# A Conformer convolution inside a decoder trunk: first weights split ahead and kept in DRAM, tap matrices from the host, fewer TensorE taps

## The chip, the cores and the metric

The kernel runs on one core of one Trainium2 chip. The time is device microseconds of one execution; a kernel's time is the median of several executions. Five engines run beside each other: TensorE (PE, with its weight loads shown as PEld), VectorE (DVE), ScalarE (ACT), GpSimd (POOL) and SyncE (SP), which here only issues DMAs. ACT and POOL issue DMAs too.

## The reference, cut to what matters

Two layers over 512 tokens of width 1024: a Mamba-2 mixer (SSD), then a Conformer convolution module, each followed by a gated MLP with a causal convolution of width 3. The Conformer module is what the change is about:

```python
def conformer_conv(x, pw1_w, pw1_b, dw_w, dw_b, ln_g, ln_b, pw2_w, pw2_b):
    h = jax.nn.glu(x @ pw1_w + pw1_b, axis=-1)      # 1024 -> 2 x 1024
    h = causal_dwconv(h, dw_w, dw_b)                # 31 taps per channel
    h = jax.nn.silu(layer_norm(h, ln_g, ln_b))
    return h @ pw2_w + pw2_b                        # 1024 -> 1024
```

## The kernel before, in words

Activations lie channels by tokens: eight tiles of 128 channels x 512 tokens. Every product is made of three fp32r matmuls: weights and activations are split into a high part (rounded to fp32r) and a low part (the rest), and high x high, low x high and high x low are added up in PSUM (lines 275 to 277, in `mm_unit`).

Weights come as a stream of 440 units (`weight_units`), each two 128-row blocks of 256 columns. `Weights._make` (line 101) loads raw fp32 by a DMA on SP (line 110, 512 KB for two units), rounds the high part on POOL (line 115) and subtracts it on DVE for the low part (line 116). There are three raw buffers and five pairs of high and low tiles; `get` makes four units ahead of the one in use. One unit is twelve matmuls.

The order of the work: SSD, first conv FFN (`ffn(0)`: 22 up-projections of four units, in three parts, with the down-projections of each part behind it), Conformer, second FFN. The program is written in that order, and a scheduler at build time, which simulates a timeline, settles the order of instructions in each engine's queue and puts in the waits. On the chip each queue is then worked off in that order.

The Conformer (line 660 on) goes over eight channel tiles p:

- `taps(p)` (line 673) builds on DVE the small diagonal matrices with which TensorE makes taps 1 to 4J of the causal convolution, J = `PE_J[p]` (4, 4, 5, 5, 5, 5, 5, 6). They lie in half of a buffer (`ab`) of the SSD.
- `mm_pair("pw1", p, ...)` makes both halves of the GLU: 48 matmuls.
- `glu(p)` (line 685) evacuates them (`scaled`, line 304, two DVE operations), makes the sigmoid on ACT and the product `ta` on DVE (line 688). For TensorE's taps it needs four copies of `ta` that are shifted by 0 to 3 tokens: for p below 7 `ta` goes to DRAM and comes back in four DMAs from POOL's queue (lines 691 and 693); for p = 7 sixteen copies on ACT and DVE make it (lines 699 to 705). Taps 0 and above 4J are made on ACT (lines 709, 710) and DVE (line 713, one operation a tap), and added (line 716).
- `dwconv(p)` (line 719) runs TensorE's taps: for each j four matmuls of 128 x 32 in fp32, each two records in the trace (line 723). Then DVE adds them (line 728), subtracts the mean of tile 0 (line 735), and adds the tile to the sums `s1` (line 741) and of squares (line 258). It is called three tiles late, behind the last unit of pw1 of tile p + 3; the last four, tiles 4 to 7, lie behind the last pw1 matmuls.

Then three idle matmuls (line 757) keep TensorE busy, sixteen records of one-column matmuls turn the two sums (line 762), the statistics are spread over the partitions (`across`, line 767), and the second pointwise product (pw2) begins.

Of the kernel before, what the change touches and what calls it, by code (L numbers as in the profile page):

```python
# [10 lines left out]
F32 = mybir.dt.float32  # L11
F32R = mybir.dt.float32r
AF = mybir.ActivationFunctionType
ALU = mybir.AluOpType
# [3 lines left out]
P = 128  # L18
T = 512
# [7 lines left out]
CK = 31  # L27
NCH = 4
RMS_EPS = 1e-6
LN_EPS = 1e-5  # L30
PE_J = (4, 4, 5, 5, 5, 5, 5, 6)
MAX_J = 7
FPARTS = ((0, 8), (8, 16), (16, 22))

_COLS = {}
# [1 line left out]
for _name, _w in (  # L37
# [3 lines left out]
    ("fb1", 44), ("wt", 8 * MAX_J * 4),  # L41
):
    _COLS[_name] = _n
    _n += _w
# [47 lines left out]
class Weights:  # L92
    def __init__(self, nc, src, raw, split, look):
        self.nc, self.src, self.raw, self.split, self.look = nc, src, raw, split, look
        self.seq = weight_units()
        self.made = 0
        self.used = 0
        self.ready = deque()
        self.cur = None

    def _make(self):
        nc = self.nc
        kind, p, k = self.seq[self.made]
        if self.cur is None or self.cur[0] != (kind, p) or not self.cur[1] <= k < self.cur[2]:
            n = 1
            while n < (2 if self.made > 1 else 1) and self.made + n < len(self.seq) and self.seq[self.made + n] == (kind, p, k + 2 * n):
                n += 1
            t = self.raw.tile([P, 4, 256], F32, name="wraw", tag="wraw")
            s = self.src[kind][p]
            nc.sync.dma_start(t[:, 0 : 2 * n, :], s[:, k : k + 2 * n, :])  # L110
            self.cur = ((kind, p), k, k + 2 * n, t)
        t = self.cur[3][:, k - self.cur[1] : k - self.cur[1] + 2, :]
        hi = self.split.tile([P, 2, 256], F32R, name="whi", tag="whi")
        lo = self.split.tile([P, 2, 256], F32R, name="wlo", tag="wlo")
        nc.gpsimd.tensor_scalar(hi, t, 1.0, 1.0, op0=ALU.mult, op1=ALU.mult)  # L115
        nc.vector.tensor_tensor(lo, t, hi, op=ALU.subtract)  # L116
        self.ready.append((hi, lo))
        self.made += 1
# [13 lines left out]
def trunk(ctx, tc, a, out):  # L132
    nc = tc.nc
    pe, act, dve, pool = nc.tensor, nc.scalar, nc.vector, nc.gpsimd
# [8 lines left out]
    dr = ctx.enter_context(tc.tile_pool(name="dr", bufs=1, space=DRAM))  # L143
# [59 lines left out]
    def col(name, i, n=1):  # L203
        c = _COLS[name] + i
        return par[:, c : c + n]
# [99 lines left out]
            us.append(u)  # L305
        return us

    # ---------------------------------------------------------------- SSD
    sq = SqSum()
    xs = []  # L310
    dps = c_tile()
# [303 lines left out]
        ps = mm_pair("out", p, ysplit, 8, 16)  # L615
        out_evac(p, ps)

    # ---------------------------------------------------------------- conv FFN
    def ffn(i, finish, last=None):
        fx, fsq = hs["xs"], hs["sq"]  # L620
        box = {}

        def get_r():
            box["r"] = fsq.rstd(D)

        for pi, (pa, pb) in enumerate(FPARTS):
            acts = Acts()
            for p in range(pa, pb):
                ps = mm_pair(f"up{i}", p, fx, hooks={3: get_r} if p == 0 else None)
                us = scaled(ps, box["r"])  # L630
                os_ = []
                for u, j in zip(us, (p, NF + p)):
                    o = cv_tile()
                    act.activation(o, u, AF.Identity, scale=col(f"fw{i}", 3 * j + 2), bias=col(f"fb{i}", j))  # L634
                    os_.append(o)
                for d in (1, 2):
                    for u, o, j in zip(us, os_, (p, NF + p)):
                        dve.scalar_tensor_tensor(  # L638
                            o[:, d:], in0=u[:, : T - d], scalar=col(f"fw{i}", 3 * j + 2 - d), in1=o[:, d:],
                            op0=ALU.mult, op1=ALU.add,  # L640
                        )
                act.activation(os_[0], os_[0], AF.Silu)  # L642
                dve.tensor_tensor(os_[0], os_[0], os_[1], op=ALU.mult)  # L643
                acts.add(os_[0])
            for p in range(4):
                if last and pb == NF and p == 3:
                    last(acts, pa, pb)
                    break
                ps = mm_pair(f"dn{i}", p, acts, pa, pb)
                for m in range(2):  # L650
                    dve.tensor_tensor(h[2 * p + m], h[2 * p + m], ps[m], op=ALU.add)  # L651
                if pi == len(FPARTS) - 1:
                    if p == 0:
                        hs["sq"], hs["xs"] = SqSum(), []
                    for m in range(2):
                        finish(2 * p + m)

    ffn(0, lambda m: h_done(m, lambda i: col("nm1", i)))

    # ---------------------------------------------------------------- Conformer  # L660
    cx, csq = hs["xs"], hs["sq"]
    gd = [dr.tile([P, 4 + T], F32, name=f"gd{i}") for i in range(3)]
    for t in gd:
# [6 lines left out]
    ys = []  # L670
    m0s1 = wt("xdt", (P, NCH, 256), bufs=1).rearrange("p c e -> p (c e)")

    def taps(p):
        n = 4 * PE_J[p]
        if p % 3 == 0:
            box["wd"] = ab_tile().rearrange("p h t -> p (h t)")
        c = (p % 3) * 2 * T
        wd = box["wd"][:, c : c + 32 * n].rearrange("p (n e) -> p n e", e=32)
        dve.tensor_tensor(
            wd, mask32.unsqueeze(1).broadcast_to([P, n, 32]),  # L680
            col("wt", 4 * MAX_J * p, n).unsqueeze(2).broadcast_to([P, n, 32]), op=ALU.mult,
        )
        return wd

    def glu(p, ps, wd):
        ta, tb = scaled(ps, box["r"])
        act.activation(tb, tb, AF.Sigmoid, bias=col("p1b", 8 + p))
        dve.scalar_tensor_tensor(ta, in0=ta, scalar=col("p1b", p), in1=tb, op0=ALU.add, op1=ALU.mult)
        t = ap_.tile([P, 4, T], F32, name="as", tag="as")
        if p < 7:  # L690
            nc.gpsimd.dma_start(gd[p % 3][:, 4:], ta)
            for s in range(4):
                nc.gpsimd.dma_start(
                    t[32 * s : 32 * s + 32], gd[p % 3][:, s : s + T].rearrange("(b c) t -> c b t", b=4)
                )
        else:
            for s in range(4):
                dve.memset(t[32 * s : 32 * s + 32, :, 0 : 4 - s], 0.0)
            for b in range(4):
                for s in range(4):  # L700
                    o, i = t[32 * s : 32 * s + 32, b, 4 - s :], ta[32 * b : 32 * b + 32, : T - 4 + s]
                    if s % 2:
                        act.activation(o, i, AF.Copy)
                    else:
                        dve.tensor_copy(o, i)
        acc = [cv_tile(), u_tile()]
        dw = lambda d: col("dw", CK * p + CK - 1 - d)
        d2 = 4 * PE_J[p] + 1
        act.activation(acc[0], ta, AF.Identity, scale=dw(0), bias=col("dwb", p))
        act.activation(acc[1][:, d2:], ta[:, : T - d2], AF.Copy, scale=dw(d2))  # L710
        for i, d in enumerate(range(d2 + 1, CK)):
            o = acc[i % 2]
            dve.scalar_tensor_tensor(  # L713
                o[:, d:], in0=ta[:, : T - d], scalar=dw(d), in1=o[:, d:], op0=ALU.mult, op1=ALU.add
            )
        dve.tensor_tensor(acc[0][:, d2:], acc[0][:, d2:], acc[1][:, d2:], op=ALU.add)
        return p, t, wd, acc[0]

    def dwconv(p, t, wd, acc):
# [9 lines left out]
        if p == 0:  # L729
# [2 lines left out]
            m0 = m0s1[:, 0:T]  # L732
            act.activation(m0, mp, AF.Copy, scale=1.0 / P)
            box["m0"] = m0
        dve.tensor_tensor(y, y, box["m0"], op=ALU.subtract)
        if p == 0:
            box["s1"] = m0s1[:, T : 2 * T]
            act.activation(box["s1"], y, AF.Copy)
            box["sq"] = SqSum()
        else:  # L740
            dve.tensor_tensor(box["s1"], box["s1"], y, op=ALU.add)
        box["sq"].add(y)
        ys.append(y)

    pend = deque()
    for p in range(8):
# [10 lines left out]
    idle(3)  # L757

    stp = c_tile()
    for i, t in enumerate((box["s1"], box["sq"].t)):  # L760
        for c in range(NCH):
            pe.matmul(
                stp[:, 4 * i + c : 4 * i + c + 1], lhsT=t[:, c * P : (c + 1) * P], rhs=ones[:, 0:1],
                start=True, stop=True,
            )

    def across(v):
# [150 lines left out]
def _layout(i):  # L918
# [15 lines left out]
    for l in range(2):  # L934
# [2 lines left out]
    o["pw1"] = _pairs(f["b_pw1_w"][0], [(P * p, D + P * p) for p in range(8)])  # L937
    o["pw2"] = _pairs(f["b_pw2_w"][0], seq4)
    dww = f["b_dw_w"][0]
    taps = dww[CK - 1 - np.arange(1, 4 * MAX_J + 1)].reshape(MAX_J, 4, 8, 4, 32)[:, ::-1]  # L940
    parts = {
        "nm0": _chan(f["norm_mix"][0]), "nm1": _chan(f["norm_mix"][1]),
        "nf0": _chan(f["norm_ffn"][0]), "nf1": _chan(f["norm_ffn"][1]),
# [4 lines left out]
        "lng": _chan(f["b_ln_g"][0]), "lnb": _chan(f["b_ln_b"][0]), "p2b": _chan(f["b_pw2_b"][0]),  # L948
        "fw0": _taps(f["f_conv_w"][0]), "fb0": _chan(f["f_conv_b"][0]),
        "fw1": _taps(f["f_conv_w"][1]), "fb1": _chan(f["f_conv_b"][1]),  # L950
        "wt": taps.transpose(1, 4, 2, 0, 3).reshape(P, -1),
    }
    o["par"] = np.ascontiguousarray(np.concatenate([parts[k] for k in _COLS], axis=1))
    o["g0"] = np.ascontiguousarray(parts["nm0"])
# [22 lines left out]
```

## Time and profile before

| what | us |
|---|---|
| median of three runs (1345.31 to 1346.75) | 1346.13 |
| span of the profiled execution, first to last instruction | 1344.2 |
| the difference, taken as what lies around the span | 1.9 |
| TensorE busy in that span | 1325.3 (99%) |
| VectorE busy | 1006.6 (75%) |
| ScalarE busy | 407.7 (30%) |
| GpSimd busy | 360.8 (27%) |

The profile is of one execution. Busy time of TensorE is taken from matmuls whose ends are modelled, so its 99% does not say that each stretch is bounded by it; where in the span something else sets the pace is read from the timelines of a stretch. DVE operations overlap by a little: from start to start of two that follow each other is less than the duration of one.

### The profile page before, as it was taken

To read this page: it belongs to the slowest core of one execution; us is meant where nothing else is said; L and a number is where in the kernel's file an instruction comes from. 1 tells how busy PE (TensorE), PEld (TensorE's weight loads), DVE (VectorE), ACT (ScalarE), POOL (GpSimd) and SP (SyncE) were. 2 spreads that over 40 slices of the span, in tenths; PEclk is the share of its full clock that TensorE was granted. 3 is DMA by queue.
4 is the path that set the end of the run, shared out by engine and by line. 5 is a ranking of instruction groups with operands and counts; after the bars stand their busy time and mean duration, and the time that the engine had idled before them with its cause. 6 is when DMAs were issued, how large, how long until landed. Compare 5 with 4: busy or idle time off the path is not lost.

```text
span 1344.2 us, 17019 instructions
## 1 busy us (share of the span) xinstructions
PE 1325.3 (99%) x6312; PEld 1069.5 (80%) x6312; DVE 1006.6 (75%) x1505; ACT 407.7 (30%) x653; POOL 360.8 (27%) x479
## 2 busy tenths in 40 slices
PE   8999999999999999999999999998999999999998
PEld 5778888888888888888888887645888888888887
DVE  7879987388989975477457779998787637763774
ACT  4575644055312321022002331225232202210224
POOL 3213222222223222222222225430222222222220
PEclk9999999999999999999999999998999999999999
DMA  6334432243233333223322336540323322232232
GB/s 215 115 125 157 157 125 94 79 138 114 95 111 108 110 95 94 94 97 100 101 95 86 100 104 188 152 131 17 110 91 98 94 95 94 96 108 94 94 87 71
DMA packets 43795, 145.55 MB, mean 108 GB/s; under 512 B 5953, under 2 KB 6337, under 8 KB 42689
## 3 DMA queue, kind: packets, MB, share of 16 engines
q1 hardware_dynamic: 40336, 135.28, 31.4%
q0 software_dynamic: 2800, 9.18, 2.7%
q8 instruction: 50, 0.82, 0.3%
q14 instruction: 33, 0.26, 0.1%
q10 hardware_dynamic: 576, 0.01, 0.0%
HBM read 140.37 MB, written 4.07 MB: 107 GB/s over the span
## 4 chain that ended last, share of the span: by engine, by line
PE 81%; DVE 12%; DMA 2%; issue 2%; ACT 2%; SPq 0%; POOL 0%; DVEq 0%; ACTq 0%; POOLq 0%
PE mm L277 26%; PE mm L275 26%; PE mm L276 25%; DVE cv L713 2%; DVE u L713 2%; DVE wlo L116 2%; DVE cv L401 1%; DMA wraw<-in_dram 1%; DMA ab<-acs_d 1%; PE pc L477 1%; DVE u L304 1%; ACT ab L444 1%; PE pc L500 1%; PE pc L473 1%; DVE sqs L258 0%
## 5 line engine op out<-in xcount | busy, mean ns | idle before, releaser
L115 POOL TENSOR_SCALAR whi<-wraw 128x512 fp32r<-128x512 f32 x440 | 340.7, 775 | 929.0 <-PE mm L277 623.9
L116 DVE TENSOR_TENSOR wlo<-wraw,whi 128x512 fp32r<-128x512 f32 x440 | 308.9, 705 | 238.6 <-POOL whi L115 237.8
L275 PE MATMUL mm<-xs,whi 128*128 128x512 f32 x1216 | 476.3, 393 | 1.1 <-POOL whi L115 0.6
L276 PE MATMUL mm<-xs,wlo 128*128 128x512 f32 x1216 | 474.4, 391 | 0.2 <-DVE wlo L116 0.2
L277 PE MATMUL mm<-xs,whi 128*128 128x512 f32 x1216 | 473.3, 391 | 0.5 <-DVE xs L222 0.5
L275 PEld LDWEIGHTS mm<-xs,whi 128*128 128x128 f32 x1216 | 228.2, 188 | 54.7 <-POOL whi L115 4.6
L276 PEld LDWEIGHTS mm<-xs,wlo 128*128 128x128 f32 x1216 | 228.2, 188 | 50.0 <-issue 1.8
L277 PEld LDWEIGHTS mm<-xs,whi 128*128 128x128 f32 x1216 | 228.0, 188 | 50.1 <-DVE xs L222 1.6
L275 PE MATMUL mm<-as,whi 128*128 128x512 f32 x532 | 207.0, 390 | 0.7 <-ACT as L242 0.7
L276 PE MATMUL mm<-as,wlo 128*128 128x512 f32 x532 | 206.8, 389 | 0.0
L277 PE MATMUL mm<-as,whi 128*128 128x512 f32 x532 | 203.8, 390 | 0.6 <-DVE as L244 0.6
L634 ACT ACTIVATE cv<-u,par 128x512 f32<-128x512 f32 x88 | 67.1, 809 | 360.9 <-DVE u L304 360.9
L638 DVE SCALAR_TENSOR_TENSOR cv<-u,par,cv 128x511 f32<-128x511 f32 (+1 forms) x176 | 136.4, 835 | 0.0
L304 DVE TENSOR_TENSOR u<-mm,rstd 128x512 f32<-128x512 f32 x152 | 102.1, 686 | 29.3 <-PE mm L277 29.3
L275 PEld LDWEIGHTS mm<-as,whi 128*128 128x128 f32 x532 | 99.9, 188 | 22.0 <-issue 1.2
L277 PEld LDWEIGHTS mm<-as,whi 128*128 128x128 f32 x532 | 99.8, 188 | 21.9 <-DVE as L244 1.0
L276 PEld LDWEIGHTS mm<-as,wlo 128*128 128x128 f32 x532 | 99.9, 188 | 20.5
L401 DVE SCALAR_TENSOR_TENSOR cv<-u,par,cv 128x511 f32<-128x511 f32 (+2 forms) x96 | 76.3, 820 | 3.1 <-ACT cv L397 2.8
L642 ACT ACTIVATE cv<-cv 128x512 f32<-128x512 f32 x44 | 27.8, 633 | 81.3 <-DVE cv L638 81.3
L651 DVE TENSOR_TENSOR h<-h,mm 128x512 f32<-128x512 f32 x46 | 30.8, 686 | 24.6 <-PE mm L277 24.6
L218 ACT ACTIVATE as<-cv 128x512 fp32r<-128x512 f32 x44 | 27.9, 634 | 67.7 <-DVE cv L643 67.7
L444 ACT ACTIVATE ab<-ab,acT 128x128 f32<-128x128 f32 x128 | 38.9, 389 | 15.5 <-DMA ab<-acs_d 15.5
(181 smaller groups left out, 943.4 us busy)
## 6 DMA issues: line engine op xcount, KB each, us to landing
wraw<-up_dram SPq DMA_DIRECT2D x88, 512.0 KB, 3.6
wraw<-in_dram SPq DMA_DIRECT2D x47, 512.0 KB, 3.7
wraw<-dn_dram SPq DMA_DIRECT2D x40, 512.0 KB, 3.6
wraw<-pw_dram SPq DMA_DIRECT2D x24, 512.0 KB, 3.7
ab<-acs_d SPq DMA_DIRECT2D x8, 1024.0 KB, 4.9
wraw<-out_dram SPq DMA_DIRECT2D x16, 512.0 KB, 3.9
as<-gd POOLq DMA_DIRECT2D x28, 256.0 KB, 5.5
ab<-nac_d SPq DMA_DIRECT2D x32, 128.0 KB, 5.9
```

What stands on the lines that cost most here:

```text
L115: nc.gpsimd.tensor_scalar(hi, t, 1.0, 1.0, op0=ALU.mult, op1=ALU.mult)
L116: nc.vector.tensor_tensor(lo, t, hi, op=ALU.subtract)
L275: pe.matmul(ps[m], lhsT=whi[:, kk, c], rhs=xhi, start=(k + kk == k0), stop=False)
L276: pe.matmul(ps[m], lhsT=wlo[:, kk, c], rhs=xhi, start=False, stop=False)
L277: pe.matmul(ps[m], lhsT=whi[:, kk, c], rhs=xlo, start=False, stop=(k + kk == k1 - 1))
L304: dve.tensor_tensor(u, q, r, op=ALU.mult)
L401: dve.scalar_tensor_tensor(o[:, d:], in0=u[:, : T - d], scalar=col("cw", 4 * i + 3 - d), in1=o[:, d:], op0=ALU.mult, op1=ALU.add,)
L444: act.activation(e, e, AF.Relu, bias=acT[:, c, 4 * g + j : 4 * g + j + 1], scale=-1.0)
L634: act.activation(o, u, AF.Identity, scale=col(f"fw{i}", 3 * j + 2), bias=col(f"fb{i}", j))
L638: dve.scalar_tensor_tensor(o[:, d:], in0=u[:, : T - d], scalar=col(f"fw{i}", 3 * j + 2 - d), in1=o[:, d:], op0=ALU.mult, op1=ALU.add,)
L651: dve.tensor_tensor(h[2 * p + m], h[2 * p + m], ps[m], op=ALU.add)
L713: dve.scalar_tensor_tensor(o[:, d:], in0=ta[:, : T - d], scalar=dw(d), in1=o[:, d:], op0=ALU.mult, op1=ALU.add)
```

## The change

- `PE_J` becomes (4, 4, 4, 4, 4, 4, 4, 5): 33 instead of 39 steps of four tap matmuls on TensorE; the other taps go to DVE (line 713).
- `presplit`: during the first FFN, behind its tiles 5 to 21, sixteen parts of pw1's weights (512 KB each) are loaded into the SSD's `ab` buffers, split on ACT (high) and DVE (low), and written to DRAM from POOL's queue, 1 MB a part. In the Conformer, `_make` then loads high and low directly, two DMAs of 256 KB a unit on SP, with no work on POOL and DVE.
- `taps(p)` loads the diagonal matrices, made on the host, by a DMA from POOL's queue instead of building them on DVE.
- The shifted copies of tile 7 are sixteen DMAs on SP from SBUF to SBUF.
- The mean of tile 0 is subtracted before TensorE's taps are added for p above 2 (line 735's operation moves into `glu`), and tile 7 is left out of the two sums: four more matmuls each on the tile and on its square take their place.

```diff
-PE_J = (4, 4, 5, 5, 5, 5, 5, 6)
+PE_J = (4, 4, 4, 4, 4, 4, 4, 5)
...
+        if kind in self.split_src:
+            pair = []
+            for q, name in enumerate(("whi", "wlo")):
+                t = self.split.tile([P, 2, 256], F32R, name=name, tag=name)
+                nc.sync.dma_start(t.rearrange("p k c -> p (k c)").bitcast(F32), self.split_src[kind][p][:, k // 2, q, :])
+                pair.append(t)
+            self.ready.append(tuple(pair))
+            self.made += 1
+            return
...
+    def presplit(kind, n):
+        W.split_src[kind] = [dr.tile([P, 4, 2, T], F32, name=f"{kind}s{p}", tag=f"{kind}s{p}") for p in range(n)]
+        parts = [(p, k) for p in range(n) for k in (0, 4)]
+        b = None
+        for i in range(len(parts) + 1):
+            prev = b
+            if i < len(parts):
+                p, k = parts[i]
+                b = ab_tile()
+                nc.sync.dma_start(b[:, 0:2, :].rearrange("p u (k c) -> p (u k) c", k=2), a[kind][p][:, k : k + 4, :])
+            if prev is not None:
+                p, k = parts[i - 1]
+                o = prev[:, 2:6, :].rearrange("p (u q) t -> p u q t", q=2)
+                r = o.bitcast(F32R)
+                for u in range(2):
+                    act.activation(r[:, u, 0, :], prev[:, u, :], AF.Copy)
+                    dve.tensor_tensor(r[:, u, 1, :], prev[:, u, :], r[:, u, 0, :], op=ALU.subtract)
+                nc.gpsimd.dma_start(W.split_src[kind][p][:, k // 2 : k // 2 + 2], o)
+            yield
...
+        ahead = presplit("pw1", 8) if i == 0 else iter(())
...
+                if p > 4:
+                    next(ahead, None)
...
-        dve.tensor_tensor(
-            wd, mask32.unsqueeze(1).broadcast_to([P, n, 32]),
-            col("wt", 4 * MAX_J * p, n).unsqueeze(2).broadcast_to([P, n, 32]), op=ALU.mult,
-        )
+        nc.gpsimd.dma_start(wd, a["wd"][:, 128 * sum(PE_J[:p]) : 128 * sum(PE_J[: p + 1])])
...
-                dve.memset(t[32 * s : 32 * s + 32, :, 0 : 4 - s], 0.0)
-            for b in range(4):
-                for s in range(4):
-                    o, i = t[32 * s : 32 * s + 32, b, 4 - s :], ta[32 * b : 32 * b + 32, : T - 4 + s]
-                    if s % 2:
-                        act.activation(o, i, AF.Copy)
-                    else:
-                        dve.tensor_copy(o, i)
+                pool.memset(t[32 * s : 32 * s + 32, :, 0 : 4 - s], 0.0)
+            for s in range(4):
+                for b in range(4):
+                    nc.sync.dma_start(t[32 * s : 32 * s + 32, b, 4 - s :], ta[32 * b : 32 * b + 32, : T - 4 + s])
...
+        if p > 2:
+            dve.tensor_tensor(acc[0], acc[0], box["m0"], op=ALU.subtract)
...
-        dve.tensor_tensor(y, y, box["m0"], op=ALU.subtract)
+        if p < 3:
+            dve.tensor_tensor(y, y, box["m0"], op=ALU.subtract)
...
-        else:
+        elif p < 7:
             dve.tensor_tensor(box["s1"], box["s1"], y, op=ALU.add)
-        box["sq"].add(y)
+        if p < 7:
+            box["sq"].add(y)
...
-    for i, t in enumerate((box["s1"], box["sq"].t)):
+    sq7 = wt("sq", bufs=2)
+    act.activation(sq7, ys[7], AF.Square)
+    for j, t in enumerate((box["s1"], box["sq"].t, ys[7], sq7)):
```

## Rows read from the trace of the kernel before

**Rows 1.** The page's head: span and number of instructions.
```profile
span 1344.2 us, 17019 instructions
```
**Rows 2.** Busy time by stretch: PE, PEld, DVE, ACT, POOL, clock, DMA share, GB/s.
```profile
405.00:783.00 378.00, 378.00 (x1668) 312.62 (x1667) 266.50 (x383) 80.15 (x118) 102.15 (x139) 1.00 0.31 98
783.00:890.00 107.00, 107.00 (x534) 76.79 (x532) 100.21 (x141) 23.92 (x34) 46.48 (x62) 1.00 0.55 151
```
**Rows 3.** Timeline of PE: start, us, line, operation, tiles, shape, count.
```profile
889.73 0.39 PE L277 MATMUL mm<-xs,whi 128*128 128x512 f32 x1
890.04 8.66 PE L723 MATMUL pc<-as,ab 128*32 128x512 f32 x80
...
912.54 2.84 PE L175 MATMUL mm<-con,ones 128*128 128x512 f32 x6
919.35 1.36 PE L762 MATMUL pc<-ones,xdt 128*128 128x1 f32 x8 [3.97 <-DVE xdt L741]
920.57 1.84 PE L762 MATMUL pc<-ones,sqs 128*128 128x1 f32 x8
```
**Rows 4.** Timeline of DVE in the Conformer.
```profile
799.68 1.27 DVE L304 TENSOR_TENSOR u<-mm,rstd 128x512 f32<-128x512 f32 x2
801.94 0.75 DVE L688 SCALAR_TENSOR_TENSOR u<-u,par 128x512 f32<-128x512 f32 x1
803.57 1.36 DVE L713 SCALAR_TENSOR_TENSOR cv<-u,par,cv 128x494 f32<-128x494 f32 x1 [0.89 <-ACT cv L709]
804.86 0.72 DVE L713 SCALAR_TENSOR_TENSOR u<-u,par 128x493 f32<-128x493 f32 x1
805.50 0.72 DVE L713 SCALAR_TENSOR_TENSOR cv<-u,par,cv 128x492 f32<-128x492 f32 x1
...
896.43 0.68 DVE L304 TENSOR_TENSOR u<-mm,rstd 128x512 f32<-128x512 f32 x1
...
901.37 0.74 DVE L688 SCALAR_TENSOR_TENSOR u<-u,par 128x512 f32<-128x512 f32 x1
...
919.23 0.69 DVE L258 TENSOR_TENSOR sqs<-sqs,sq 128x512 f32<-128x512 f32 x1
```
**Rows 5.** Groups of DVE instructions from 783 to 922 us.
```profile
L713 DVE SCALAR_TENSOR_TENSOR cv<-u,par,cv 128x486 f32<-128x486 f32 (+6 forms) x42 | 34.2, 823 | 0.9 <-ACT cv L709 0.9
L116 DVE TENSOR_TENSOR wlo<-wraw,whi 128x512 fp32r<-128x512 f32 x33 | 23.6, 719 | 5.7 <-POOL whi L115 5.7
L705 DVE COPY as<-u 32x508 f32<-32x508 f32 (+1 forms) x8 | 3.3, 415 | 0.1
L679 DVE TENSOR_TENSOR ab<-con,par 128x640 f32<-128x640 f32 (+1 forms) x2 | 2.0, 1022 | 0.0
```
**Rows 6.** Timeline of POOL: a rounding beside the long DVE operation of rows 4.
```profile
803.77 0.63 POOL L115 TENSOR_SCALAR whi<-wraw 128x512 fp32r<-128x512 f32 x1
```
**Rows 7.** Groups of instructions of the whole span.
```profile
L219 DVE TENSOR_TENSOR as<-cv,as 128x512 fp32r<-128x512 f32 x44 | 30.4, 691 | 0.8 <-ACT as L218 0.7
L218 ACT ACTIVATE as<-cv 128x512 fp32r<-128x512 f32 x44 | 27.9, 634 | 67.7 <-DVE cv L643 67.7
L437 PEld LDWEIGHTS pc<-con,cv 128*128 128x128 f32 x64 | 7.4, 141 | 0.3
```
**Rows 8.** Timeline of SP: four loads issued one behind the other.
```profile
5.60 2.08 SPq L190 DMA_DIRECT2D cv<-x_dram  x4
```
**Rows 9.** DMA issues: KB each, median us to landing (820 to 880 us; whole span).
```profile
as<-gd POOLq DMA_DIRECT2D x16, 256.0 KB, 5.3
...
y_dram<-u SPq DMA_DIRECT2D x8, 256.0 KB, 2.3
```
**Rows 10.** DMA queues from 820 to 880 us: packets, MB, share of 16 engines.
```profile
q0 software_dynamic: 1810, 5.91, 39.3%
q1 hardware_dynamic: 1150, 4.19, 24.8%
```
**Rows 11.** Busy time by stretch, columns as in rows 2: the clock around the statistics.
```profile
920.00:922.00 2.00, 2.00 (x11) 2.00 (x11) 0.00 (x0) 0.50 (x1) 0.00 (x0) 0.50 0.00 0
```

More of the change, by code (lines that the diff above doesn't have):

```diff
@@ L30 @@
 LN_EPS = 1e-5
-PE_J = (4, 4, 5, 5, 5, 5, 5, 6)
-MAX_J = 7
+PE_J = (4, 4, 4, 4, 4, 4, 4, 5)
 FPARTS = ((0, 8), (8, 16), (16, 22))
@@ L40 @@
     ("lng", 8), ("lnb", 8), ("p2b", 8), ("fw0", 132), ("fb0", 44), ("fw1", 132),
-    ("fb1", 44), ("wt", 8 * MAX_J * 4),
[1 row of a table added]
 ):
@@ L99, in __init__ @@
         self.cur = None
+        self.split_src = {}
     def _make(self):
@@ L677, in taps @@
         c = (p % 3) * 2 * T
-        wd = box["wd"][:, c : c + 32 * n].rearrange("p (n e) -> p n e", e=32)
-        dve.tensor_tensor(
-            wd, mask32.unsqueeze(1).broadcast_to([P, n, 32]),
-            col("wt", 4 * MAX_J * p, n).unsqueeze(2).broadcast_to([P, n, 32]), op=ALU.mult,
-        )
-        return wd
+        wd = box["wd"][:, c : c + 32 * n]
+        nc.gpsimd.dma_start(wd, a["wd"][:, 128 * sum(PE_J[:p]) : 128 * sum(PE_J[: p + 1])])
+        return wd.rearrange("p (n e) -> p n e", e=32)
     def glu(p, ps, wd):
@@ L734, in dwconv @@
             box["m0"] = m0
-        dve.tensor_tensor(y, y, box["m0"], op=ALU.subtract)
+        if p < 3:
+            dve.tensor_tensor(y, y, box["m0"], op=ALU.subtract)
+        ys.append(y)
         if p == 0:
@@ L739, in dwconv @@
             box["sq"] = SqSum()
-        else:
+        elif p < 7:
             dve.tensor_tensor(box["s1"], box["s1"], y, op=ALU.add)
-        box["sq"].add(y)
-        ys.append(y)
+        if p < 7:
+            box["sq"].add(y)
     pend = deque()
@@ L759, in trunk @@
     stp = c_tile()
-    for i, t in enumerate((box["s1"], box["sq"].t)):
+    sq7 = wt("sq", bufs=2)
+    act.activation(sq7, ys[7], AF.Square)
+    for j, t in enumerate((box["s1"], box["sq"].t, ys[7], sq7)):
         for c in range(NCH):
+            i = 4 * (j % 2) + c
             pe.matmul(
-                stp[:, 4 * i + c : 4 * i + c + 1], lhsT=t[:, c * P : (c + 1) * P], rhs=ones[:, 0:1],
-                start=True, stop=True,
+                stp[:, i : i + 1], lhsT=t[:, c * P : (c + 1) * P], rhs=ones[:, 0:1],
+                start=(j == 0 and c == 0), stop=(j == 3 and c == NCH - 1), skip_group_check=True,
             )
@@ L939, in _layout @@
     dww = f["b_dw_w"][0]
-    taps = dww[CK - 1 - np.arange(1, 4 * MAX_J + 1)].reshape(MAX_J, 4, 8, 4, 32)[:, ::-1]
+    wd = []
+    for p, nj in enumerate(PE_J):
+        w4 = dww[CK - 1 - np.arange(1, 4 * nj + 1), P * p : P * (p + 1)].reshape(nj, 4, 4, 32)[:, ::-1]
+        d = np.zeros((4, 32, nj, 4, 32), np.float32)
+        for c in range(32):
+            d[:, c, :, :, c] = w4[:, :, :, c].transpose(1, 0, 2)
+        wd.append(d.reshape(P, -1))
+    o["wd"] = np.ascontiguousarray(np.concatenate(wd, axis=1))
     parts = {
@@ L950, in _layout @@
         "fw1": _taps(f["f_conv_w"][1]), "fb1": _chan(f["f_conv_b"][1]),
-        "wt": taps.transpose(1, 4, 2, 0, 3).reshape(P, -1),
     }
```

1 row of the table _n is left out of this document.

## The prediction

> **What bounds the kernel now.** I read the page's head first: a span of 1344.2 us [rows 1], which with the 1.9 us of the table around it makes 1346.1, the median. Its 99% of TensorE says little, so I went to the table by stretch. In the first FFN, 405 to 783 us, TensorE is busy for all 378 us, DVE for 266, ACT for 80, POOL for 102, the DMA engines for 31% [rows 2]: TensorE sets the pace and everything else has room. From 783 to 890 us, the first pointwise product, TensorE is again full, though DVE works 100 of 107 us.
>
> The third view, the timelines from 890 us on, shows the loss. The last pw1 matmul ends at 890.1; TensorE's taps of tiles 4 to 7 and the idle matmuls follow, and then TensorE stands still for 3.97 us until DVE has made the sum, and the statistics run to 922.4 [rows 3]. DVE has worked without a stop from 799.7 to 919.9 [rows 4]. It is behind: tile 7's evacuation comes at 896.4, 6.3 us after its product was there, and the product `ta` only at 902.1 [rows 3, 4]. So at this place DVE's backlog is what ends last, and the change's worth is read here: when do the statistics end? All else is beside TensorE's work.
>
> **The first FFN.** Presplit adds sixteen parts. Each costs two roundings on ACT (0.63 us) and two subtractions on DVE (0.69) [rows 7], one load issue on SP and one store issue on POOL: some 20 us on ACT and 22 on DVE in a stretch where they have 298 and 111 to spare [rows 2]. The bytes, 8.4 MB read and 16.8 written, over some 270 us (seventeen up-projection tiles at 10.9 and thirty-two units of down-projection at 2.7) add 93 GB/s to 98, so the DMA share about doubles to 0.6. I cost it at nothing: the cover is TensorE's full queue and the weights made four units, 10.9 us, ahead. What could break it: POOL's store waits for DVE, and roundings of the next weights are queued behind it. A wait longer than those 10.9 us would show at once as idle TensorE. Bounds: 0, and an estimated 1 us for each of sixteen parts.
>
> **TensorE in the Conformer.** Forty tap records take 8.66 / 2 = 4.33 us [rows 3], 0.108 each. `PE_J` loses 39 - 33 = 6 steps of eight records, 5.2 us. Before the last pw1 matmul lie tiles 0 to 3 with two of those steps, so pw1 ends 1.7 us earlier, at 888.4; tiles 4 to 6 then take 3 x 3.46 = 10.4 us, to 898.8.
>
> **DVE in the Conformer.** Operations start 0.60 to 0.64 us apart, as at 804.86 and 805.50 [rows 4]. Removed after 799.7: of the 33 low parts [rows 5] six lie before 799.7 and five belong to pw2, 22 x 0.60 = 13.2 us; two builds of tap matrices, 2.0; the copies of tile 7, 3.3 [rows 5]; tile 7's two sums, 1.2. Also POOL's roundings: the tap at 803.57 took 1.36 us instead of 0.72, and beside it lies a rounding of 0.63 [rows 4, 6]. Over all 42 + 34 taps the mean is 0.82 (the row of the 42) against 0.72, 7.6 us, of which I give pw1's roundings 6. The Trainium skill (SBUF — State Buffer, Who interferes with whom) says that a DVE instruction with two SBUF inputs and a GpSimd instruction that reads SBUF exclude each other. By that alone 22 roundings would have cost DVE up to 13.9 us, and DVE would end 8 us earlier than below; the mean over the taps says that mostly they missed each other. Added: 24 taps, 24 x 0.64 = 15.4 us. Net 25.7 - 15.4 = 10.3 us: DVE ends at 919.9 - 10.3 = 909.6.
>
> **Tile 7's way.** Its lag of 6.3 us should be gone, since most of the 10.3 us lie before it. From evacuation to `ta` it took 3.0 us for tile 0 undisturbed and 5.7 for tile 7 [rows 4]; I take 4.3: `ta` at 892.7. Then sixteen DMAs are issued on SP: four loads took 2.08 [rows 8], so 16 x 0.52 = 8.3 us, to 901.0. The trace has no SBUF-to-SBUF transfer; the nearest are 2.3 us for the stores of the output and 5.3 for the gathers from DRAM [rows 9]; I take 2.3, as the queue is nearly empty then: 903.3. TensorE's taps of tile 7, forty records, 4.3: 907.6. TensorE has 4.5 us to wait there, from 898.8. The scheduler simulates this wait and has three idle matmuls that depend on nothing: I take it that they fill 2.84 us of it [rows 3], so that the clock stays up. Without that the wait is longer than the 3.97 us of standing still after which the granted clock was 0.50, 1.2 GHz [rows 3, 11]; that is a rival.
>
> **The end.** DVE's last addition (909.6) comes later than the taps. A square on ACT, 0.6: 910.2. The statistics are now thirty-two records instead of sixteen. Before, sixteen took 3.1 us, at half clock [rows 3, 11]. At 2.4 GHz a weight load of this kind took 0.141 us [rows 7], so thirty-two take 4.5. The sixteen on the two older sums go between 907.6 and 910.2, beside DVE's last work; sixteen are left: 910.2 + 2.3 = 912.5, where it was 922.4, so 9.9 us less. The spreading of the statistics behind it ran at half clock too; at full clock I estimate 1.2 us less, half of 2.4 us in which it held the path. What follows on ACT, DVE and pw2 stays.
>
> **The sum.** 1344.2 - 9.9 - 1.2 = 1333.1; with 1.9 around it 1335.0. Bounds of the unknown costs: 5.3 for the landing moves the taps' end to 910.6 and the end to 911.2 + 4.5 = 915.7, 3.2 more; an issue of 0.33 a DMA would change nothing, as DVE ends later; the presplit 0 to 16 more.
>
> **The rivals.** *The tail is shorter.* DVE loses the whole 13.9 us to POOL today and ends by 902; `ta` comes at 891.5, the taps of tile 7 end at 906.4 and the statistics at 906.4 + 1.2 + 2.3 = 909.9: 12.5 + 1.2 less, 1332.4; with issues of 0.33 on SP 3 us less again, 1329.4. For it: DVE never rests in the whole stretch. Against: the mean of the taps.
>
> *The shift is late and cold.* SP's sixteen issues stand behind waiting weight loads, or the idle matmuls stay behind the taps, where they are now [rows 3]. TensorE then stands still past the 3.97 us, and tile 7's taps take 8.7 us at half clock: 903.3 + 8.7 = 912.0, addition and square 913.2, statistics 4.5 to 6: about 918.5, 3.9 less: 1342.2.
>
> *The first FFN gives it back.* Stores on POOL's queue delay roundings: at 0.5 us a part 8 us come back, 1345.4, no change. Against: 276 us of idle POOL there [rows 2].
>
> *The weights starve, slower.* From 783 to 888 some 25.2 MB must move: 14.7 MB of weights (twice the bytes), seven tiles' shifted copies at 1.31, 1.3 of tap matrices. That is 240 GB/s. From 820 to 880 the software queue moved 5.91 MB in 39.3% of 60 us and the hardware queue 4.19 in 24.8% [rows 10]: 251 and 282 GB/s if they had all engines. At 251 it just fits (100 us of 105). The gain of 11.1 us is used up when pw1 takes that much more, below 25.2 MB / 116 us = 217 GB/s; at 205, 123 us, pw1 ends 18 us later: 1335.0 + 18 = 1353. For it: the first three tiles have no taps and ask for (2.1 + 1.31) / 10.9 = 313 GB/s. Against: DVE spaces the gathers by 13 us or more, and the weights run ahead. The Trainium skill (DMA: Bandwidth & Descriptors, Bandwidth) speaks against this edit too: transfers below 1 MiB fall short of the peak, and these are 256 KB. No row here shows such a shortfall for loads that follow each other.
>
> That the change does not do what it says I rule out: DVE's and POOL's work on pw1's weights leaves the Conformer by construction.
>
> **How the numbers follow.** Forecast 0.47, shorter tail 0.18, late shift 0.16, given back 0.08, starving 0.11. About 0.2%, 2.7 us, is what a measurement here can tell from no change, so faster means below 1343.4: 0.47 + 0.18 + 0.16 = 0.81; same 0.08; slower 0.11. The range from 1329.5 (the shorter tail with its fast issues) to 1343.0 (the late shift and a little) leaves out about 0.2. The likeliest is 1335.0.
>
> **What would show it.** In the stretch 405 to 783 TensorE stays full and its length within 1 us; no rounding of pw1 on POOL; taps on DVE near 0.72 us. The last pw1 matmul ends near 888, `ta` of tile 7 near 893, sixteen SP issues take about 8 us, the statistics end near 912 at full clock. I am wrong if pw1's matmuls wait for DMAs, if TensorE's first FFN has gaps, or if DVE is idle for long in the Conformer while the end stays.

## The result, and the profile after: slower by 0.9%, where 0.8% faster was forecast

The changed kernel takes 1358.45 us (median of 4 runs, 1355.05 to 1358.81) against 1345.74 (1345.31 to 1346.75) for the kernel before on the same chip: a ratio of 1.0089, with a 95% interval of 1.0074 to 1.0103. The forecast was 1335.0, with a range to 1343.0: wrong in sign and outside its range.

The first reading is where the two traces part. DVE evacuates every product pair by the same multiplication (line 304 before, 313 after), so the n-th one can be paired with the n-th, and the difference of their starts says how much later it comes:

| the evacuation at, in the kernel before | where that is | after, minus before |
|---|---|---|
| 348.3 us | near the end of the SSD | -0.4 |
| 443.6 | first tile of the first FFN | +12.4 |
| 467.2 | fourth tile | +20.0 |
| 499.8 | seventh tile | +18.4 |
| 750.1 | end of the first FFN | +15.4 |
| 989.1 | second FFN | +12.3 |
| 1299.5 | last tile | +12.2 |

The values of 18 to 20 are in part DVE's own lateness; TensorE's matmuls, paired in the same way, are 12.9 us late from 448 us on and 15.3 from 487. So 15.8 us (from -0.4 to +15.4) are lost around the start of the first FFN, which the forecast had at nothing, and the Conformer wins 3.1 of the 11.1 that it was to win. The page's head of the changed kernel [rows 1]:

```profile
span 1356.6 us, 17117 instructions
```

With the 1.85 us of the profiled execution around its span that is the median, 1358.45. Its table by stretch (columns as in [rows 2]):

```profile
405.00:500.00 95.00, 86.19 (x358) 68.94 (x356) 87.93 (x123) 36.33 (x58) 32.45 (x43) 0.95 0.77 265
500.00:783.00 283.00, 281.32 (x1240) 232.80 (x1241) 186.29 (x270) 51.49 (x75) 78.67 (x110) 1.00 0.34 106
...
798.50:902.40 103.90, 103.90 (x518) 76.13 (x516) 91.26 (x139) 24.16 (x34) 24.92 (x45) 1.00 0.86 240
```

TensorE stands still for 8.8 + 1.7 = 10.5 us in a stretch where it was full before [rows 2], and the granted clock is 0.95 in the first part, which by an estimate costs up to 0.05 x 95 = 4.8 us more. The traffic shows what else is different from the forecast: 265 GB/s until 500 us and 106 after it. All sixteen parts are split between 358 and 498 us, eleven of them before the first FFN's first evacuation (456.0), and none behind tiles 5 to 21, where the source has them. The order on the queues is the scheduler's, and it moved them ahead.

The waits of that stretch, 354 to 505 us (engine, line, what it waited for: us in total, times, longest):

```profile
ACT ab L642 <- DMA ab<-pw_dram: 40.9, 11, 8.6
...
POOL pw1s L644 <- DVE ab L643: 34.9, 9, 5.9
...
DVE ab L643 <- ACT ab L642: 10.1, 7, 2.3
...
SPq L636 <- DMA pw1s<-ab: 40.5, 11, 8.3
...
PE mm L284 <- DVE u L313: 6.5, 1, 6.5
```

The first four are one wait handed round: ACT's rounding waits for the load of a part, DVE's subtraction for ACT, POOL's store for DVE, and SP's next load but one for that store to land, since there are two `ab` buffers. Each of them stands in an in-order queue, so what is behind it waits too. TensorE's longest wait, from the timelines of SP, ACT, DVE, POOL and PE (start, us, engine, line):

```profile
448.26 0.33 SPq L636 DMA_DIRECT2D ab<-pw_dram  x1
...
453.42 1.15 ACT L642 ACTIVATE ab<-ab 128x512 fp32r<-128x512 f32 x2 [2.33 <-DMA ab<-pw_dram]
...
451.61 3.35 DVE L274 RECIPROCAL rstd<-rstd 128x512 f32<-128x512 f32 x1
454.87 1.22 DVE L643 TENSOR_TENSOR ab<-ab 128x512 fp32r<-128x512 f32 x2
456.01 2.47 DVE L313 TENSOR_TENSOR u<-mm,rstd 128x512 f32<-128x512 f32 x4
...
456.39 0.58 POOL L644 DMA_DIRECT2D pw1s<-ab  x1 [5.42 <-DVE ab L643]
...
449.35 1.02 PE L271 MATMUL pc<-sqs,ones 128*128 128x512 f32 x2
456.84 0.77 PE L284 MATMUL mm<-xs,whi 128*128 128x512 f32 x1 [6.47 <-DVE u L313]
```

TensorE waits 6.47 us for the evacuation (456.01) to free a bank and starts slower (0.77 us for a matmul that else takes 0.39). The part's own wait is here, 2.33 us on ACT for the load of 448.26, but DVE was still at the reciprocal when ACT was done; of the 6.47 us only the subtractions between reciprocal and evacuation, 1.1, are the part's. The evacuation needs the norm, and the sums of squares for it came to TensorE at 449.35, 11.4 us later than in the kernel before (437.98). So it is to be asked what made DVE late before that. From the first row of the table to the second, the kernel before and the changed one (columns as in [rows 2]):

```profile
348.28:443.58 95.30, 95.30 (x462) 78.88 (x461) 88.30 (x126) 23.07 (x37) 27.67 (x32) 1.00 0.34 111
...
347.84:456.01 108.17, 100.40 (x472) 81.54 (x470) 99.22 (x143) 36.07 (x59) 34.83 (x43) 0.97 0.73 253
```

The stretch is 12.9 us longer; DVE works 10.9 us more in it and rests 2.0 us more (9.0 instead of 7.0). With none of the parts there (the run with the wait taken out, below) DVE works 82.45 us of 94.07 from the one evacuation to the other: it would rest 11.6 us, and with the parts it works 16.8 us more. So at this place the parts' work on DVE is itself without room, beside the waits.

The tail of the Conformer, timelines of PE, SP and DVE; [rows 3, 4, 8] answer to them, 15.4 us earlier:

```profile
902.14 0.39 PE L286 MATMUL mm<-xs,whi 128*128 128x512 f32 x1
902.46 10.39 PE L750 MATMUL pc<-as,ab 128*32 128x512 f32 x96
912.78 2.84 PE L184 MATMUL mm<-con,ones 128*128 128x512 f32 x6
918.76 1.89 PE L750 MATMUL pc<-as,ab 128*32 128x512 f32 x2 [3.14 <-DMA as<-u]
920.58 1.87 PE L794 MATMUL pc<-ones,xdt 128*128 128x1 f32 x8
922.38 1.92 PE L750 MATMUL pc<-as,ab 128*32 128x512 f32 x4
924.23 1.87 PE L794 MATMUL pc<-ones,sqs 128*128 128x1 f32 x8
926.02 7.29 PE L750 MATMUL pc<-as,ab 128*32 128x512 f32 x34
...
935.01 1.03 PE L794 MATMUL pc<-ones,sq 128*128 128x1 f32 x8
...
908.95 10.06 SPq L730 DMA_DIRECT2D as<-u  x16
...
908.18 0.74 DVE L717 SCALAR_TENSOR_TENSOR u<-u,par 128x512 f32<-128x512 f32 x1
...
922.01 0.69 DVE L743 TENSOR_TENSOR cv<-cv,xdt 128x512 f32<-128x512 f32 x1
933.35 0.69 DVE L755 TENSOR_TENSOR cv<-cv,pc 128x512 f32<-128x512 f32 x1 [10.65 <-PE pc L750]
```

DVE is done at 922.7 and then waits 10.65 us for TensorE: it no longer sets the end. Tile 7's product is there at 908.9, its sixteen transfers are issued from 908.95 to 919.0, and TensorE, after the idle matmuls, stands still for 3.14 us; then forty tap records take 1.89 + 1.92 + 7.29 = 11.1 us instead of 4.3, with sixteen statistics records between them (3.7 us). The granted clock there (table by stretch):

```profile
918.80:926.00 7.20, 7.20 (x22) 3.86 (x22) 3.83 (x6) 0.00 (x0) 0.00 (x0) 0.50 0.08 19
```

### The profile page after: what moved, and what is told of

Read it like the earlier page. It is cut to its first block, busy times and chain, and to the rows that moved or that the text cites. A ratio compares the mean times of both kernels' runs of the same rounds, so it can differ in the third digit from the quotient of the medians.

```text
span 1356.6 us, 17117 instructions
## 1 busy us (share of the span) xinstructions
PE 1328.9 (98%) x6280; PEld 1071.6 (79%) x6280; DVE 1005.6 (74%) x1507; ACT 421.3 (31%) x677; POOL 352.4 (26%) x475
## 4 chain that ended last, share of the span: by engine, by line
PE 83%; DVE 7%; DMA 4%; issue 2%; ACT 2%; SPq 1%; POOL 0%; DVEq 0%; ACTq 0%; POOLq 0%
PE mm L286 25%; PE mm L284 25%; PE mm L285 25%; DMA ab<-pw_dram 2%; PE pc L750 2%; DVE wlo L125 1%; PE pc L486 1%; DMA pw1s<-ab 1%; DVE cv L410 1%; PE pc L509 1%; DMA wraw<-in_dram 1%; PE pc L482 1%; DVE u L313 1%; DVE ab L643 1%; SPq L730 1%
## 5 line engine op out<-in xcount | busy, mean ns | idle before, releaser
L124 POOL TENSOR_SCALAR whi<-wraw 128x512 fp32r<-128x512 f32 x408 | 318.9, 783 | 841.7 <-PE mm L286 547.5
L125 DVE TENSOR_TENSOR wlo<-wraw,whi 128x512 fp32r<-128x512 f32 x408 | 289.4, 712 | 224.6 <-POOL whi L124 223.8
L664 ACT ACTIVATE cv<-u,par 128x512 f32<-128x512 f32 x88 | 67.2, 809 | 348.3 <-DVE u L313 348.3
```

## Experiments on the first FFN: what made 15 us of it

**One part behind each tile.** If the hoisting alone did the harm, tying each load to its tile cures it: one column of the tile's output is copied into the buffer that the load fills, so that the load cannot go ahead.

```
 b = ab_tile()
+act.activation(b[:, 0, 0:1], gate[0][:, 0:1], AF.Copy)
 nc.sync.dma_start(b[:, 0:2, :]..., a[kind][p][:, k : k + 4, :])
```

> The changed kernel, with each presplit part tied to its own tile of the first FFN: one column of its buffer is written from that tile's result before the load, so the scheduler cannot put the load ahead of it (an ACT copy of 128x1 a part is added). Theory A (place): the 15.4 us by which pw1 starts late come from all sixteen parts standing between 354 and 498 us, where DVE has no room; spread over tiles 5 to 21 they cost nothing, pw1 starts near 783 to 784, total 1358.4 - 15 = 1343 us. Rival A' (load): the parts cost TensorE their time wherever they stand (stores that hold POOL's queue, bytes on the DMA engines): pw1 still starts at 791 or later, total 1350 or more.

Measured: 1384.29 us (1377.74 to 1385.88), ratio 1.0282 [1.0256, 1.0307]. The parts cost more where the source has them: 40.4 us are lost by the end of the first FFN. Timelines of ACT, DVE and POOL in one period of its trace:

```profile
616.86 0.19 ACT L638 ACTIVATE ab<-cv 128x1 f32<-128x1 f32 x1
622.42 1.16 ACT L645 ACTIVATE ab<-ab 128x512 fp32r<-128x512 f32 x2 [5.38 <-DMA ab<-pw_dram]
...
623.09 0.69 DVE L646 TENSOR_TENSOR ab<-ab 128x512 fp32r<-128x512 f32 x1 [3.61 <-ACT ab L645]
...
625.29 0.58 POOL L647 DMA_DIRECT2D pw1s<-ab  x1 [12.07 <-DVE ab L646]
625.90 2.36 POOL L124 TENSOR_SCALAR whi<-wraw 128x512 fp32r<-128x512 f32 x4
```

Here the chain stands bare. The load is issued at 617.08, the roundings stand next on ACT's queue and wait 5.38 us for it, DVE waits 3.61, POOL's store 12.07, and behind the store stand the roundings of four weight tiles, which then come in one burst. TensorE gets its weights late (it waits 3.3 us for the low part at 615.75), the next tile and so the next load come late, and the period is 15 us (the next two stores are at 640.07 and 655.2) where a tile took 10.9.

**The same place, the wait taken out.** The load is tied to its tile as above; the roundings are tied to the *next* tile, by a bias of zero made from that tile's output. When they come up on ACT's queue, the load has landed.

```
+z = gz[:, i : i + 1]
+act.activation(z, gate[0][:, 0:1], AF.Copy, scale=0.0)
 for u in range(2):
-    act.activation(r[:, u, 0, :], prev[:, u, :], AF.Copy)
+    act.activation(r[:, u, 0, :], prev[:, u, :], AF.Identity, bias=z)
```

> The changed kernel with each part's load tied to one tile of the first FFN and its roundings tied to the next tile (a bias of zero worked out from that tile's result), so that a load has 10.9 us before anything waits for it. In the run with only the load tied, the roundings stood right behind their own load: ACT waited 5 us a part for it, DVE for ACT, POOL's store for DVE 12 us, and four roundings of weights behind the store. Theory C (queues): it is this wait, handed from queue to queue, that stops TensorE, not the work or the bytes; with loads a tile ahead the first FFN is as before, pw1 starts at 783 to 786, and the total is 1358.4 - 15 = 1343 to 1345 us. Rival C' (work): DVE's and ACT's added operations and the bytes stop it; pw1 starts 8 us late or more, total 1351 or more.

Measured: 1341.71 us (1340.8 to 1344.24), ratio 0.9979 [0.997, 0.9989]. The first FFN's loss is gone: -0.28 us at 467, at 500 and at 750 us. The same bytes, the same operations and one small one more a part, beside the same tiles as in the run before, cost nothing (table by stretch):

```profile
480.00:520.00 40.00, 40.00 (x179) 33.10 (x178) 32.55 (x48) 12.81 (x24) 12.17 (x16) 1.00 0.47 151
520.00:600.00 80.00, 80.00 (x355) 66.24 (x354) 47.90 (x71) 14.46 (x26) 22.93 (x34) 1.00 0.50 166
600.00:783.00 183.00, 183.00 (x809) 151.54 (x808) 132.74 (x197) 52.96 (x97) 57.01 (x80) 1.00 0.62 208
```

A part on the timelines of ACT and POOL of the same run:

```profile
626.25 0.19 ACT L646 ACTIVATE gz<-cv 128x1 f32<-128x1 f32 x1
626.47 1.34 ACT L648 ACTIVATE ab<-ab,gz 128x512 fp32r<-128x512 f32 x2
...
629.05 0.58 POOL L650 DMA_DIRECT2D pw1s<-ab  x1
```

The rounding at 626.47 shows no wait in brackets, nor does the store at 629.05, and TensorE is full in every stretch. What cost 40 us one run earlier, beside these tiles, was the wait and not the work.

**The stores on ACT's queue.** The changed kernel, with only `nc.gpsimd.dma_start(W.split_src...)` made `nc.scalar.dma_start(...)`.

> The changed kernel with presplit's stores issued from ACT's queue instead of POOL's; the scheduler still puts the parts where it likes. Theory C1 (POOL): the stores, which wait up to 5.9 us for DVE with weight roundings behind them, are the main cause: the loss in the first FFN falls from 15.4 to below 6 us, total 1349 or less. Theory C2 (DVE and ACT): the waits of ACT for the loads and of DVE for ACT, ahead of the evacuations and low parts, are the main cause: the loss stays within 3 us of 15.4, total 1355 to 1362.

Measured: 1354.19 us (1351.58 to 1355.87), ratio 1.0068 [1.0051, 1.0084]; the loss is within the second expectation, the time just below it. In the profiled execution, the fastest of the four, the offset grows by 12.5 us around the start of the first FFN (-1.5 to +10.9) instead of 15.8: stores on POOL's queue are at most about a fifth of the loss. The waits of DVE for ACT are not the rest: until the first evacuation they come to 0.8 us here, against 5.7 in the changed kernel, and that stretch is hardly shorter (table by stretch, against the two rows above):

```profile
346.75:454.25 107.50, 99.20 (x472) 80.19 (x470) 99.82 (x144) 35.49 (x59) 29.70 (x33) 0.99 0.75 258
```

TensorE's longest wait is the same one, 6.26 us for DVE's evacuation. DVE's added work, 11.5 us more than before, is what is left as the main term there; no run takes it away alone.

**No split ahead.** `ahead = iter(())` for `presplit("pw1", 8)`: pw1 loads its weights raw, as before; all else of the change stays.

> The changed kernel without presplit: pw1's weights are rounded on POOL and DVE in the Conformer, as before; the tap matrices from the host, the fewer TensorE taps and tile 7's DMAs stay. Theory A: the first FFN is as before (pw1 starts near 783), but DVE gets 13 us of low parts and the taps stretched by roundings back on top of 24 more taps: its end moves some 15 us later than in a paced presplit, total 1353 to 1358 us. Rival (DVE is not what ends last, the shift by DMA is): the Conformer is as long as in the changed kernel, 142 us from the first pw1 to the first pw2 matmul, total 1343.

Measured: 1355.43 us (1354.22 to 1356.33), ratio 1.0076 [1.0061, 1.0091]. The first FFN then loses nothing (the offset is 1.2 us at 348 and 1.1 at 750), but the Conformer loses 8.3: the other edits without the split make it slower.

## Experiments on the tail: what became of the Conformer's gain

**The shift by copies again,** as in the kernel before, sixteen copies on ACT and DVE in turn; all else as changed.

> The changed kernel with tile 7 shifted by the sixteen copies on ACT and DVE, as before, instead of sixteen DMAs on SP; all else, presplit too, stays as changed. Theory B (issue): the DMAs are issued one behind the other, 0.63 us each, 10 us in all, and the wait halves TensorE's clock for tile 7's taps (918.8 to 933.3 us); with copies (5 us, before) the statistics end some 10 to 12 us earlier, total 1347 us. Rival B' (DVE): DVE, with 24 more taps, sets the end, and the copies come on top of it: total 1358 or more.

Measured: 1356.4 us (1355.83 to 1357.38), ratio 1.0082 [1.0065, 1.0099]. The first FFN lost 16.6 here (+1.3 to +17.9), so the Conformer wins 7.2 instead of 3.1: the direct DMAs cost 4 us against the copies. It is not more because DVE, with 24 more taps and the copies, is then late: TensorE waits twice 2.4 us for its last sums. With the parts tied to their tiles as well:

> Both: presplit tied to its tiles, tile 7 shifted by copies. Theories A and B, independent of each other: 1358.4 - 15 - 11 = 1332 us, faster than the kernel before by some 13 us. If the two losses hide one another, not below 1340.

Measured: 1379.2 us (1373.6 to 1380.06), ratio 1.0244 [1.0222, 1.0266]: the loss of the first run is in it (+38.5 us at the end of the first FFN), and the Conformer wins 6.5.

**Two queues for the shift.** The kernel with the wait taken out, and every second transfer of tile 7 on POOL's queue: `(nc.sync if s % 2 else nc.gpsimd).dma_start(...)`.

> The fully tied presplit, and tile 7's sixteen DMAs shared between SP and POOL, eight each. Theory B (issue): eight issues take 5 us instead of 10, the shift lands some 5 us earlier, TensorE's wait gets short enough for the full clock, and DVE's end (7.5 us before the taps' end in the changed kernel) becomes the bound: 9 to 12 us less than the run with one queue, 1332 to 1335 us. Rival: POOL's own issues and landings are slower than SP's, and less than 4 us are won.

Measured: **1334.71 us** (1334.27 to 1335.45), ratio 0.9925 [0.991, 0.994]: 7.0 us below the same kernel with one queue, and the fastest of all. Timelines of PE, SP, POOL and DVE:

```profile
888.60 0.39 PE L286 MATMUL mm<-xs,whi 128*128 128x512 f32 x1
888.92 10.39 PE L757 MATMUL pc<-as,ab 128*32 128x512 f32 x96
899.24 2.84 PE L184 MATMUL mm<-con,ones 128*128 128x512 f32 x6
902.01 5.28 PE L757 MATMUL pc<-as,ab 128*32 128x512 f32 x40
...
910.91 1.03 PE L801 MATMUL pc<-ones,sq 128*128 128x1 f32 x8
...
895.40 5.07 SPq L737 DMA_DIRECT2D as<-u  x8
...
895.67 3.99 POOL L737 DMA_DIRECT2D as<-u  x8 [5.97 <-DVE u L724]
...
909.26 0.69 DVE L762 TENSOR_TENSOR cv<-cv,pc 128x512 f32<-128x512 f32 x1
```

The issues take 5.1 us instead of 10.1 and end at 900.5, all but the last four transfers land while the idle matmuls run, tile 7's taps follow without a break at a granted clock of 1.00, and TensorE waits only 0.84 us for DVE's last addition. The Trainium skill (DMA: Bandwidth & Descriptors, Issuing engines are not separate DMA queues) says that starting DMAs from several engines saves only the time on the sequencer, usually small beside the DMA itself. That it is the issue time which is saved agrees; here that time was the larger one, 10.06 us of issues against 2.0 us from the last issue to its landing.

**Late, or cold?** The one-queue kernel with the wait taken out, and six more idle matmuls ahead of tile 7's taps, so that TensorE does not stand still.

> The gated kernel (all shifts on SP, 1341.7) with six more idle matmuls ahead of tile 7's taps, 0.47 us each, so that TensorE works from 897.2 to some 905.7 us instead of standing still for 3.15 and running tile 7's taps at the clock of 1.2 GHz. Theory cold (the standing still costs more than itself, because the taps and the statistics behind it go at half clock): the forty taps take 5.3 us instead of some 10 us with their breaks, tile 7's sum comes near 912 instead of 917.7, 1335 to 1337.5. Theory late (the sixteen issues of 10.1 us on SP and their landing are the loss, whatever the clock): the last transfer lands at about 905.5 in both, the taps end where the transfers let them, 1339.5 to 1342.

Measured: 1338.83 us (1338.02 to 1342.68), ratio 0.9957 [0.994, 0.9974]: 2.9 us of the 7.0, between the two theories. Its timeline of PE:

```profile
897.70 7.99 PE L184 MATMUL mm<-con,ones 128*128 128x512 f32 x18
905.62 1.04 PE L757 MATMUL pc<-as,ab 128*32 128x512 f32 x2
...
909.33 4.41 PE L757 MATMUL pc<-as,ab 128*32 128x512 f32 x34
```

The thirty-four records go at 0.13 us instead of 0.21, so the clock was a good third of the loss; the rest, by difference, is put down to the lateness of the sixteen issues and the statistics still between the taps.

**The split ahead, priced with the tail repaired.** No split ahead, and the shift on two queues.

> The changed kernel without the split ahead (pw1's weights are loaded raw and split on POOL and DVE beside it, as before), with tile 7's shift on two queues: all that is left of the change but its first part, with the repaired tail. Theory DVE (the split ahead is what pays, since it takes 19 us of work and of port conflicts from DVE in a stretch that DVE ends): without it DVE ends 10 to 15 us later than in the gated kernel on two queues, near 922 us or after it, and the time is 1345 to 1352, no better than before. Theory tail (the queues of the shift are what pays, and DVE is not what ends last): 1335 to 1339.

Measured: 1356.12 us (1355.85 to 1356.67), ratio 1.0081 [1.0065, 1.0098]: slower than either theory had it. DVE works without a stop until its last sum here:

```profile
925.33 0.68 DVE L267 TENSOR_TENSOR sqs<-sqs,sq 128x512 f32<-128x512 f32 x1
...
912.43 7.23 PE L750 MATMUL pc<-as,ab 128*32 128x512 f32 x40 [4.10 <-DMA as<-u]
924.96 1.84 PE L794 MATMUL pc<-ones,xdt 128*128 128x1 f32 x8 [5.30 <-DVE xdt L770]
```

It ends at 926.0, against 909.95 with the split on two queues; less their offsets at the end of the first FFN (-0.67 and +1.75) that is 18.5 us, and all thirty-two statistics then come behind it at a granted clock of 0.50 (925 to 932 us). Two queues bring nothing without the split (1355.43 with one), and the split brings 21 with two.

**The taps.** The two-queue kernel with `PE_J` of the kernel before (4, 4, 5, 5, 5, 5, 5, 6), and with one between (4, 4, 4, 4, 5, 5, 5, 5):

> The gated kernel on two queues (1334.7) with the kernel before's division of the taps, 4, 4, 5, 5, 5, 5, 5, 6: TensorE takes six more steps of eight records (5.2 us), DVE 24 taps less (some 15 us). Theory DVE is then no bound and tile 7's way sets the end: pw1 ends 1.7 us later, tile 7's taps take 1.0 us more, and its product comes up to 2 us sooner behind pw1: 1334 to 1338, so the fewer taps bring next to nothing. Theory TensorE (each step of taps lies on the path): 5 us more, 1339 to 1341.

> As the run before, with 36 instead of 33 tap steps on TensorE (4, 4, 4, 4, 5, 5, 5, 5): twelve taps, 7.6 us, go from DVE back to TensorE, whose taps take 2.6 us more. If DVE sets the end there, 2 to 5 us less than the run before; if tile 7's way over the shift sets it, about the same, within 2 us.

Measured: 1337.91 us (1337.28 to 1338.36), ratio 0.9944 [0.9929, 0.9959], and 1336.96 (1333.5 to 1337.2), ratio 0.9935 [0.992, 0.995]. So fewer TensorE taps bring some 3 us, once DVE has the room; the step between cannot be told from the changed division.

## Why the prediction was wrong

*The first FFN, costed at nothing: the step that failed.* The forecast took it that ACT and DVE have room for the parts, and that weights made four units ahead cover any wait. Two things were taken for granted. The place was read from the source, sixteen parts behind tiles 5 to 21; the queues had them from 358 to 498 us. There, until the first evacuation, DVE without the parts rests 11.6 us and worked 16.8 us more with them, and 12.9 of the 15.8 us were lost. And the wait was looked for at POOL alone; it goes round from load to ACT, DVE, store and the next load but one, and a load takes a median of 5.0 us to land in front of an ACT that is already waiting. Beside the tiles that the source names, the forecast's own sign came true: POOL's store waited 12.07 us, longer than the cover of 10.9, and some 40 us were lost, well past the bound of 16. That the changed kernel's 15.8 lie within this bound is luck. With the loads a tile ahead the work did fit there, at no cost (1341.71): busy shares say whether work fits into the stretch that they are taken from, and not whether a wait does.

*TensorE and pw1: right.* pw1 was to end 1.7 us earlier; it took 104.0 us from its first matmul to its end instead of 106.9, 3.0 less. Without the split it took 105.2, so 1.8 came with the other edits, as forecast, and 1.2 with the split; by what way was not followed.

*The weights starve: refuted.* TensorE was full through pw1 at 240 GB/s, what the forecast asked for, with the DMA engines at 0.86. The rule of the Trainium skill (DMA: Bandwidth & Descriptors, Bandwidth) on transfers below 1 MiB cost no time here, on loads of 256 KB that follow each other. Whether they fall short of the peak is not shown by that: 240 GB/s was what was asked for.

*DVE, net 10.3 us less: right.* It was to end at 909.6. It ended, but for tile 7's last addition, at 922.7 - 15.4 = 907.3 in the changed kernel, and with it at 909.95 - 1.75 = 908.2 in the best one. The largest terms, 13.2 for the low parts and 6 for POOL's roundings beside the taps, come to 19.2, against 18.5 measured without the split.

*Tile 7's way: the second step that failed, by terms that were too small.* The lag of `ta` behind pw1 was taken as 4.3 us and was 6.4 (902.5 to 908.9); the sixteen issues as 8.3 and were 10.06; the forty tap records as 4.3 and were 5.28 even at a granted clock of 1.00, on two queues; the landing alone was shorter, 2.0 for 2.3. The wait became 3.14 us longer than the idle matmuls, which did fill their 2.84 as forecast, and the granted clock fell to 0.50. The statistics of the older sums were put behind the taps, beside DVE's last work; on TensorE's queue sixteen of them stand between tile 7's first taps, 3.7 us at a granted clock of 0.50. The statistics ended at 936.0 - 15.4 = 920.6, 1.8 us earlier than before [rows 3], not 9.9. The rival "late and cold" had the mechanism, at 918.5.

*The chances.* Two rivals came true together, the late shift as it was described, the first FFN in another way than by POOL's stores, and the forecast had them as alternatives. They lie in different stretches, so their prices add: by its own times 1335.0 + 7.2 + 10.4 = 1352.6, outside the range and on the other side. (The 10.4 is 1345.4 - 1335.0; the 8 us that it names for this rival would give 1343.0.) The chance of slower, 0.11, was given to a third one alone.

With both repaired, the time is 1334.71 and the statistics end at 911.9 - 1.75 = 910.2, where the forecast said 1335.0 and 912.5. That the times agree so closely is in part luck: this kernel issues the shift in 5.1 us where the forecast had 8.3, the statistics end 2.3 us sooner than forecast, and what follows them gained next to nothing of the 1.2 us put down for it (12.2 us won until there, 12.5 at the next evacuation).

What stays open: how the loss in the changed kernel divides between DVE's work and the waits. Whether the parts, where the scheduler put them, would cost less without their waits was not tried; the run that took the waits out also spread the parts. The tap matrices from the host, the earlier subtraction of the mean and the sums without tile 7 were not tried one by one.

## What to carry to other kernels

Work put beside a full engine is free only under two conditions. The engine that does it has room in the very stretch where the queues have it, and no instruction of it waits at the head of an in-order queue. So read the place from the queues and not from the source, and where a scheduler orders them, tie the place with a data dependency. Look for the load that the work waits for, follow the wait from queue to queue, and let one whole step pass between a load and its first use. And price a group of small transfers on the path by issues times the time of one issue; here two queues halved that, from 10.1 to 5.1 us.

## What was not expected of the hardware

An issue on SP took 0.63 us for these transfers of 64 KB (10.06 / 16), where four loads had shown 0.52 [rows 8]; on POOL 0.50 (3.99 / 8). From SBUF to SBUF they landed 2.0 us after the issue from one queue, and 2.0 to 3.6 us after it from two.
